# A hand-ordered decoder-layer kernel: five engine queues and their buffer choices replaced by another order

## The chip, the cores and the metric

The kernel runs on one core of one Trainium2 chip. The metric is the device time of one execution in microseconds (us). The core has engines that each work through a queue of their own, in order: PE (TensorE, matrix products), DVE (VectorE), ACT (ScalarE) and POOL (GpSimd) for work on rows, and SP (SyncE), which in this kernel does nothing but start transfers (DMAs). Engines meet through semaphores: an instruction whose input is not there holds back everything that is queued behind it on its engine.

## The reference

One layer of a decoder is computed for a prompt of 512 positions and for 8 sample rows that read paged caches. Both groups share all weights. The core of it:

```python
shift, scale, gate = jnp.split(jax.nn.silu(c) @ w_ada + b_ada, 3, axis=-1)
h = x * (1.0 + scale[:, None, :]) + shift[:, None, :]
parts = jnp.split(h @ w_in, np.cumsum(IN_WIDTHS)[:-1], axis=-1)
...
o_a = nsa_attention(...)      # compressed blocks, selected blocks, window
o_b = moba_attention(...)     # top-3 blocks and the own block
y_a = (o_a.reshape(bsz, t, NSA_WIDTH) * jax.nn.silu(a_z)) @ w_up_a
y_b = (o_b.reshape(bsz, t, MOBA_WIDTH) * jax.nn.silu(b_z)) @ w_up_b
mixed = (jax.nn.sigmoid(m_a) * y_a + jax.nn.sigmoid(m_b) * y_b) @ w_out
x_new = layer_norm(DEEPNORM_ALPHA * x + gate[:, None, :] * mixed, ln_g, ln_b)
```

Two things of it matter here. Nothing can be projected before `shift` and `scale` are known, and these take the whole of `w_ada` for them (8 MB in float32). And the sample rows need scores against the selected-block cache, which lies in pages that the page table names.

## The kernel before, in words

**Numbers.** A float32 product is done as three products of a rounded format: the high part of x times the high and the low part of the weight, and the low part of x times the high part. So each weight tile that lands (`raw`) is cast by ACT to its high part and then subtracted by DVE or POOL to get the low part (`lo`, L366). In trace rows the pair of the two parts is `hl`, and of the modulated input it is `hTh` (high) and `hTl` (low).

**The head.** The modulation is computed in 8 chunks j of 128 channels. For a chunk, two 512 KB pieces of `w_ada` (named `u` or `y`, from `ada_ss`, L574) land; `ada` multiplies them with `cs`, the activated conditioning vector, in 8 small matmuls for each piece (rows s<-u,cs); ACT copies the sums (`a`), PE transposes them (s<-first_in,a), DVE reduces them to shift and scale (`ssh`), and ACT and DVE turn a 260 KB piece of x (from `xT`, names ev, z, tmp) into `hTh` and `hTl`. Then the first three weights (names kc, vc, ks in the code; raw_128, raw_140 and raw_153 from `w_cols`, 512 KB each) are multiplied with each chunk as it comes. `cs`, the identity matrix for the transposes and the bias come with one 110 KB transfer, `first_in` (L660): the constants. Where PE has nothing else, `warm` lets it multiply zeros (e<-zn, L657); 20 of these records stand in the head.

**The body.** The other projections (d<-hTh,hl) make most of PE's work. Between them the queue of PE holds the attention of the prompt (scores s<-kd,q, transposes of probabilities pt<-first_in,p, outputs) and of the sample rows. For these, tiles of selected-block pages (`raw<-slck`: 16 pages of 64 KB for one tile) are multiplied with a padded query (e<-raw,zn, L1469 and L1480 through L351), then window rows (`wink`) and block-attention pages (`mobk`, `mobv`). A page's address is read from the page table by SP itself (the rows TENSOR_LOAD and ISA between DMAs). Results of gates are stored to DRAM and loaded again later (`m_d<-mg`).

**What sets the order.** The functions write the instructions in program order; `line_up` then puts each engine's instructions in the order of a table, `QUEUES`, one string of numbers for each of the five engines, by a chain of order-only dependences. `Pool.tile` looks up in a second table, `SLOTS`, which of its buffers each new tile takes, so which earlier tile must have been used up before a load or a write may start. Waits follow from data and buffers; the tables decide only order and buffer. SP's queue carries every load, so a DMA that waits for a buffer holds back all later ones.

Of the kernel before, what the change touches and what calls it, by code (L numbers as in the profile page):

```python
# [74 lines left out]
for _name, _w in (("ident", 128), ("rowmask", 1), ("ones", 1), ("p16", 1),  # L75
# [16 lines left out]
    "ring.wr": "0123012032130213201231203130130231201302301321012303201032131023231120310",  # L92
# [4 lines left out]
    "ps.s": "01101010010101101010110011010101110101001001010101100101000101001010010111011000011000101010011000110111010110100101100110",  # L97
    "start.a": "01010110",
    "ps.d": "01201120102012000221202101202102120121022021020112120201122100201021020112102210021210211012012110211210210202100121201022112102012021220210"
        "2102",  # L100
    "ring.whl": "012012021021021020210210201201201201201201210212021200210201201201210210201201012010210121012010210210210102120",
    "phi.craw": "10230132012323010213",
# [6 lines left out]
    "at.sm": "012345670123456107234567012354673120546701235467012354670123546701235467012356470123546701235467",  # L109
# [32 lines left out]
1233-1234 1158-1169 1187-1192 1255-1256 1244-1246 1186 1247-1248 1193-1198 1213-1218 1263-1264 1271-1272 1199-1210 1227-1232 1219-1224 1249-1254
1235-1240 1257-1262 1307-1308 1279-1288 1295-1300 1289-1294 1265-1270 1273-1278 1309-1314 1345-1350 1355-1360 1301-1302 1317-1318 1331-1332 1315-1316
1319-1324 1339-1342 1325-1330 1343-1344 1333-1338 1361-1362 1351-1354 1365-1370 1385-1390 1363-1364 1303-1306 1371-1374 1395-1402 1375-1376 1403-1408
1383-1384 1451-1456 1391-1394 1377-1382 1461-1466 1409-1410 1415-1420 1449-1450 1423-1428 1421-1422 1411-1414 1493-1498 1431-1438 1429-1430 1439-1444
1507-1512 1485-1490 1457-1460 1491-1492 1445-1448 1503-1506 1475-1478 1467-1468 1529-1534 1519-1520 1555-1560 1587-1592 1499-1502 1469-1474 1513-1518
1527-1528 1521-1526 1479-1484 1561-1568 1573-1578 1595-1600 1543-1554 1539-1542 1585-1586 1603-1608 1615-1622 1601-1602 1569-1572 1627-1632 1609-1614
1583-1584 1535-1538 1579-1582 1593-1594 1635-1640 1653-1658 1661-1666 1669-1674 1633-1634 1651-1652 1623-1626 1693-1696 1675-1680 1645-1650 1667-1668
1681-1682 1641-1644 1683-1688 1705-1710 1659-1660 1697-1704 1689-1692 1737-1744 1719-1722 1745-1750 1711-1718 1727-1732 1769-1770 1754-1755 1723-1726
1771-1776 1756-1767 1751-1752 1781-1786 1793-1798 1791-1792 1733-1736 1817-1822 1831-1836 1809-1811 1753 1812-1814 1803-1808 1768 1777-1780 1823-1824  # L150
1815-1816 1787-1790 1827-1830 1851-1854 1799-1802 1855-1862 1837-1842 1825-1826 1845-1850 1879-1884 1887-1892 1885-1886 1911-1916 1843-1844 1901-1906
1909-1910 1867-1878 1897-1900 1925-1928 1863-1866 1929-1930 1945-1950 1893-1896 1919-1924 1943-1944 1907-1908 1959-1964 1917-1918 1965-1968 1931-1936
1994-1999 1937-1942 2002-2007 1992-1993 1955-1958 1969-1970 1951-1954 1988-1991 2016-2019 1977-1980 1971-1976 1987 2026-2027 1981-1986 2000-2001
2008-2009 2038-2045 2034-2037 2056-2057 2028-2033 2010-2015 2046-2051 2080-2081 2052-2055 2082-2085 2064-2067 2094-2095 2124-2125 2074-2079 2092-2093
2020-2025 2086-2091 2058-2063 2068-2073 2112-2113 2096-2101 2154-2155 2108-2111 2136-2139 2120-2123 2146-2148 2114-2119 2102-2107 2149-2151 2132-2135
2152-2153 2174-2175 2140-2145 2156-2157 2126-2131 2168-2173 2176-2181 2158-2163 2210-2211 2184-2187 2182-2183 2164-2167 2194-2197 2230-2233 2198-2209
2218-2221 2224-2229 2262-2263 2188-2193 2234-2235 2222-2223 2212-2217 2246-2251 2242-2243 2236-2241 2264-2269 2286-2291 2274-2275 2296-2301 2256-2261
2276-2281 2244-2245 2356-2361 2292-2293 2252-2255 2270-2273 2338-2343 2372-2377 2344-2349 2282-2285 2382-2387 2350-2351 2428-2433 2390-2395 2336-2337
2302-2303 2294-2295 2362-2369 2304-2335 2398-2413 2352-2355 2488-2493 2388-2389 2434-2439 2378-2381 2416-2427 2458-2463 2370-2371 2414-2415 2494-2499
2464-2469 2396-2397 2442-2453 2548-2553 2472-2483 2502-2507 2510-2515 2454-2457 2574-2579 2554-2559 2470-2471 2440-2441 2484-2487 2562-2573 2560-2561  # L160
2580-2585 2508-2509 2500-2501 2516-2547 2677-2692 2609-2620 2590-2597 2633-2634 2602-2607 2621-2626 2586-2589 2627-2632 2635-2640 2663-2664 2608
2598-2601 2651-2662 2641-2646 2780-2781 2695-2700 2665-2670 2647-2650 2719-2724 2701-2706 2671-2676 2707-2718 2725-2730 2693-2694 2766-2767 2748-2753
2731-2746 2754-2759 2798-2799 2760-2765 2788-2791 2747 2768-2773 2792-2797 2800-2805 2816-2818 2876-2877 2774-2779 2782-2787 2833-2834 2806-2815
2827-2832 2825-2826 2844-2849 2835-2840 2856-2861 2841-2842 2894-2895 2850-2851 2819-2824 2843 2862-2869 2852-2855 2888-2893 2918-2919 2896-2901
2920-2925 2870-2875 2878-2887 2936-2939 2902-2903 2930-2935 2904-2917 2940-2941 2926-2929 2964-2969 2942-2947 2956-2963 2952-2955 2948-2951 2979-2980
# [1863 lines left out]
```

## Time and profile before

| what | value |
|---|---|
| times of 3 runs | 593.89, 591.33, 590.1 us, median 591.33 us |
| the profiled execution | 590.68 us, of which its span is 588.9 us |
| busy in the span | PE 573.3 us (97%), PE weight loads 84%, DVE 51%, ACT 49%, POOL 48% |
| mean granted clock of PE | 0.988 |
| moved by DMA | 124.83 MB, 212 GB/s over the span |

The profile is of one execution. Its page gives shares over the whole span; the stages are told apart by asking the trace for stretches of time. A timeline row reads: start, duration, engine, line of the kernel, operation, output<-input, shape, how many in a row (x8), and in brackets the idle time before it with what ended that. Buffer numbers are left out of trace names, so raw<-slck stands for each of the page tiles. Line numbers are those of the kernel before; the changed file is one line longer, so each line below the tables has a number that is higher by one.

### The profile page before, as it was taken

What the parts mean: (1) busy time and instruction counts of PE and PEld (TensorE: products, weight loads), DVE (VectorE), ACT (ScalarE), POOL (GpSimd) and SP (SyncE); (2) the same over time, 40 slices, a digit from 0 to 9 for tenths busy, and PEclk for the clock granted to TensorE, in tenths of its full rate; (3) what the DMA queues carried; (4) which work ended last, traced back from release to release, by engine and by line L of the source; (5) the groups of instructions that cost most, each with busy time, mean ns of one, the idle gap of its engine ahead of it and who ended that gap; (6) DMA issues with size and microseconds to landing.
All of it is one profiled execution on the core that took longest, in us unless ns stands there. A gap on an engine that the chain in (4) does not pass through costs nothing.

```text
span 588.9 us, 13102 instructions
## 1 busy us (share of the span) xinstructions
PE 573.3 (97%) x4672; PEld 493.9 (84%) x4672; DVE 300.2 (51%) x838; ACT 289.4 (49%) x680; POOL 282.8 (48%) x313
## 2 busy tenths in 40 slices
PE   6999999999999899999999999999999999999994
PEld 3789999999997688968779898998778778889774
DVE  0676434625565475545354445775541154644485
ACT  2459455735465455644544474666443342332362
POOL 1124476563254345244425647484444246676716
PEclk7999999999999899999999999999999999999998
DMA  8978845621775834367979472860898988342413
GB/s 305 405 274 284 255 119 176 198 80 39 218 206 166 294 138 162 128 233 229 330 272 311 185 251 60 287 211 20 291 390 259 362 313 293 109 163 96 156 64 146
DMA packets 63667, 124.83 MB, mean 212 GB/s; under 512 B 8114, under 2 KB 25970, under 8 KB 63090
## 3 DMA queue, kind: packets, MB, share of 16 engines
q1 hardware_dynamic: 62194, 119.80, 59.8%
q0 software_dynamic: 1408, 4.20, 2.1%
q8 instruction: 37, 0.61, 0.4%
q14 instruction: 28, 0.23, 0.1%
HBM read 114.38 MB, written 9.58 MB: 210 GB/s over the span
## 4 chain that ended last, share of the span: by engine, by line
PE 93%; DMA 2%; DVE 1%; issue 1%; POOL 1%; SPq 1%; POOLq 0%; ACT 0%; DVEq 0%
PE d L351 55%; PE s L351 13%; PE e L351 9%; PE o L351 6%; PE pt L354 5%; PE pt L351 2%; DMA u<-ada_ss 1%; DMA raw<-slck 1%; PE d L354 1%; PE e L354 1%; PE s L354 0%; POOL p L1279 0%; SPq L357 0%; POOL hl L366 0%; SPq L574 0%
## 5 line engine op out<-in xcount | busy, mean ns | idle before, releaser
L351 PE MATMUL d<-hTh,hl 128*128 128x260 f32 (+1 forms) x1392 | 264.1, 287 | 0.0
L351 PEld LDWEIGHTS d<-hTh,hl 128*128 128x128 f32 (+1 forms) x1392 | 215.7, 188 | 2.4 <-issue 0.8
L351 PE MATMUL d<-hTl,hl 128*128 128x260 f32 (+1 forms) x704 | 198.2, 282 | 0.0
L351 PEld LDWEIGHTS d<-hTl,hl 128*128 128x128 f32 (+1 forms) x704 | 131.7, 187 | 0.0
L366 POOL TENSOR_TENSOR hl<-raw,hl 128x512 fp32r<-128x512 f32 x56 | 73.6, 1315 | 105.5 <-ACT hl L448 86.3
L1277 ACT ACTIVATE p<-s,sm 128x512 f32<-128x512 f32 (+3 forms) x96 | 50.6, 529 | 69.0 <-DVE sm L1274 45.5
L448 ACT CAST hl<-raw 128x512 fp32r<-128x512 f32 (+1 forms) x103 | 62.7, 618 | 44.2 <-PE d L351 20.2
L1279 POOL TENSOR_SCALAR p<-p,sm,gp 128x512 f32<-128x512 f32 (+3 forms) x64 | 42.8, 677 | 75.9 <-DVE sm L1278 68.9
L351 PE MATMUL d<-yh,hl 128*128 128x260 f32 x256 | 47.7, 286 | 0.0
L366 DVE TENSOR_TENSOR hl<-raw,hl 128x512 fp32r<-128x512 f32 (+1 forms) x47 | 37.1, 791 | 18.0 <-ACT hl L448 17.1
L351 PEld LDWEIGHTS d<-yh,hl 128*128 128x128 f32 x256 | 40.1, 188 | 4.0 <-issue 2.1
L354 PE MATMUL pt<-first_in,p 128*128 128x128 f32 x240 | 39.9, 281 | 0.8 <-DVE pp L1287 0.8
L354 PEld LDWEIGHTS pt<-first_in,p 128*128 128x128 f32 x240 | 27.4, 142 | 14.4 <-issue 9.0
L1287 ACT COPY pp<-pt 128x512 f32<-128x512 f32 (+1 forms) x48 | 23.0, 479 | 28.0 <-PE pt L354 27.7
L1274 DVE CUSTOM_DVE_ANT_0 s<-s,band 128x256 f32<-128x256 f32 (+1 forms) x48 | 17.3, 364 | 37.9 <-PE s L351 31.6
L351 PE MATMUL d<-yl,hl 128*128 128x260 f32 x128 | 36.2, 282 | 0.0
L1279 POOL TENSOR_SCALAR p<-p,sm,first_in 128x128 f32<-128x128 f32 (+3 forms) x32 | 23.8, 751 | 25.0 <-DVE sm L1278 24.7
L1272 DVE TENSOR_REDUCE sm<-s 128x1 f32<-128x256 f32 (+1 forms) x48 | 16.9, 355 | 33.2 <-PE s L351 27.0
L351 PE MATMUL s<-kd,q 128*128 128x512 f32 (+3 forms) x96 | 32.1, 337 | 0.0
L1287 DVE COPY pp<-pt 128x512 f32<-128x512 f32 x24 | 16.5, 688 | 28.3 <-PE pt L354 22.9
L351 PE MATMUL s<-kd,qx 128*128 128x512 f32 (+3 forms) x96 | 30.8, 323 | 0.0
L366 POOL TENSOR_TENSOR u<-craw,u 128x512 fp32r<-128x512 f32 x16 | 21.7, 1360 | 17.1 <-DMA craw<-cmp 5.9
(415 smaller groups left out, 1062.3 us busy)
## 6 DMA issues: line engine op xcount, KB each, us to landing
raw<-w_cols SPq DMA_DIRECT2D x46, 512.0 KB
raw<-mobk SPq DMA_DIRECT2D x64, 256.0 KB
raw<-mobv SPq DMA_DIRECT2D x64, 256.0 KB
craw<-cmp SPq DMA_DIRECT2D x64, 128.0 KB
u<-ada_ss SPq DMA_DIRECT2D x12, 512.0 KB
raw<-slck SPq DMA_DIRECT2D x64, 64.0 KB
raw<-ada_g SPq DMA_DIRECT2D x8, 512.0 KB
raw<-w_up SPq DMA_DIRECT2D x8, 512.0 KB
```

Of the source, the lines that this page charges most:

```text
L351: return mmraw(out, lhsT, rhs, start=start, stop=stop, skip_group_check=True)
L354: return nc.tensor.transpose(out, x, unit)
L366: (nc.gpsimd if eng == "p" else nc.vector).tensor_sub(out, x, f32(hi))
L448: nc.scalar.copy(h, src)
L1272: nc.vector.tensor_reduce(sm[:, 0:1], s[:, :b], axis=AX, op=OP.min)
L1274: nc.vector.tensor_tensor_reduce(out=s[:, b:n], in0=s[:, b:n], in1=j.band[:, 256 - (n - b):], scale=1.0, scalar=top, op0=OP.add, op1=OP.mi ...
L1277: nc.scalar.activation(pr, s[:, :n], AF.Exp, scale=-1.0, bias=sm[:, 1:2], accum_out=sm[:, 2:3])
L1279: D.setdefault("pool", []).append(nc.gpsimd.tensor_scalar(pr, pr, sm[:, 3:4], j.gate(i), op0=OP.mult, op1=OP.mult))
L1287: j.copied[gi] = (nc.scalar.copy if COPY_ENG[gi] == "a" else nc.vector.tensor_copy)(t[:, :n], p[:, :n])
```

## The change

Every instruction and every operand stays as it was. The tables `QUEUES` (all five engines) and `SLOTS` (six of its strings) hold other numbers. Cut to one of the strings and the first numbers of one queue:

```diff
 SLOTS = {
     "phi.u": "010101010100",
-    "ring.wr": "0123012032130213201231203130130231201302301321012303201032101031023231120310",
+    "ring.wr": "2013012302130210321301302102102302130321320310212303201023232103012203132",
...
 QUEUES = {
     "PE": """
-0-3 5-12 20-27 4 13 34-35 14-19 42-45 39-41 46-49 31-33 36-38 58-60 56-57 64-66 92-94 28-30 70-77 67-69 95-97 84-85 50-52 78-80 61-63 89-91 53-55
...
```

The numbers tell a reader nothing, so here is what stands in the queues.

**SP's queue at the start of the program.** `u_114` is the buffer of chunks 0 and 1 of `ada_ss` (the first two pieces are chunk 0, the next two chunk 1), `u_150` that of chunks 2 and 3; ev_136 and z_148 are the pieces of x for chunks 0 and 1. Before:

```order
L574 DMA u_114<-ada_ss 128x1024
L660 DMA first_in_72<-first 128x219
L574 DMA u_114<-ada_ss 128x1024 x3
L357 DMA raw_128<-w_cols 128x1024
L701 DMA pos_106<-pos 128x32
L357 DMA raw_140<-w_cols 128x1024
L702 DMA ptt_76<-pt 1x64
L559 DMA ev_136<-xT 128x520
L559 DMA z_148<-xT 128x520
L574 DMA u_150<-ada_ss 128x1024 x2
L357 DMA raw_153<-w_cols 128x1024
```

and now:

```order
L575 DMA u_114<-ada_ss 128x1024 x2
L358 DMA raw_128<-w_cols 128x1024
L661 DMA first_in_72<-first 128x219
L575 DMA u_114<-ada_ss 128x1024 x2
L702 DMA pos_106<-pos 128x32
L560 DMA z_148<-xT 128x520
L560 DMA ev_136<-xT 128x520
L703 DMA ptt_76<-pt 1x64
L575 DMA u_150<-ada_ss 128x1024
L358 DMA raw_140<-w_cols 128x1024
L575 DMA u_150<-ada_ss 128x1024 x2
L358 DMA raw_153<-w_cols 128x1024
```

The constants go from second to fourth place, behind another 512 KB piece of `ada_ss` and the weight raw_128; both pieces of x and the second weight change places.

**PE's queue at the start.** s_181 and s_211 are the sums of chunks 0 and 1, s_258 those of chunk 2, kd_142 is the second weight (raw_140) and v2_130 the first (raw_128). Before:

```order
L351 MATMUL e_112<-zn_90 128x256 x4
L351 MATMUL s_181<-u_114,cs_75 32x256 x8
L351 MATMUL s_211<-u_114,cs_75 32x256 x8
L351 MATMUL e_112<-zn_90 128x256 x2
L354 MATMUL s_211<-first_in_72,a_237 128x128 x2
L354 MATMUL s_181<-first_in_72,a_191 128x128 x2
L351 MATMUL e_112<-zn_90 128x256 x4
L351 MATMUL s_258<-u_150,cs_75 32x256 x4
L351 MATMUL o_251<-hTh_73,kd_142 128x260 x2
```

and now:

```order
L352 MATMUL e_112<-zn_90 128x256 x8
L352 MATMUL s_181<-u_114,cs_75 32x256 x4
L352 MATMUL s_211<-u_114,cs_75 32x256 x4
L352 MATMUL s_181<-u_114,cs_75 32x256 x4
L355 MATMUL s_181<-first_in_72,a_191 128x128 x2
L352 MATMUL s_211<-u_114,cs_75 32x256 x4
L355 MATMUL s_211<-first_in_72,a_237 128x128 x2
L352 MATMUL e_112<-zn_90 128x256 x2
L352 MATMUL d_230<-hTh_73,v2_130 128x260 x2
```

Eight of the ten products of zeros now stand ahead of everything, and the transposes of chunk 0 go between the pieces of chunk 1. (One zero product is two records in the trace; a group of 8 s<-u,cs records there is the x4 of one piece.)

**SP's queue where the last tile of selected-block pages is loaded** (raw_2783, 16 pages in four groups, each group behind a read of the page table; raw_2959, raw_2509 and raw_2721 are weight tiles, mg and ev rows that are stored). The rows with pages that only repeat are cut. Before:

```order
L357 DMA raw_2783<-slck 128x128
L357 DMA m_d_94<-mg_2504 128x520
L928 TENSOR_LOAD ptt_76
...
L357 DMA ok<-ev_2171 128x520
...
L357 DMA m_d_94<-mg_2716 128x520
L357 DMA raw_2959<-w_cols 128x1024
...
L357 DMA raw_2981<-wink 128x2048
```

and now:

```order
L358 DMA raw_2783<-slck 128x128
L358 DMA raw_2509<-w_cols 128x1024
L929 TENSOR_LOAD ptt_76
...
L358 DMA raw_2783<-slck 128x128
L358 DMA raw_2981<-wink 128x2048
L358 DMA m_d_94<-mg_2716 128x520
L358 DMA m_d_94<-mg_2944 128x520
L358 DMA band_3094<-band 128x512
L358 DMA raw_2721<-w_cols 128x1024
```

Before, a store stood behind the first group, another behind the second, and a store and a 512 KB weight behind the third, ahead of the last four pages. Now a weight stands behind the first group and nothing between the others; the store of mg_2504 stands ahead of the tile, the stores of mg_2716 and ev_2171 behind it, and so do the weights raw_2721 (which stood far ahead) and raw_2959 (now behind the store of mg_3102).

Elsewhere PE's queue is nearly the same; DVE's adds a step to `cvd_539` (L1077) ahead of the choice of selected blocks (dn, L1108) instead of behind it, and the transposes pt_4898 in PE's queue stand behind projections that they stood ahead of.

More of the change, by code (lines that the diff above doesn't have):

```diff
@@ L96 @@
     "kv.kl": "01",
-    "ps.s": "01101010010101101010110011010101110101001001010101100101000101001010010111011000011000101010011000110111010110100101100110",
+    "ps.s": "01010101101010010101001100101010001010110110100101100101000011001101101000100111100111010101011000110110101001100110100101",
     "start.a": "01010110",
[L99 to L102, printed above, removed]
+    "ps.d": "01201021012012022001202101202102120121000201202110102021100211012110201220210102210102100201201020122120120102100121200122010121201210112102"
+        "0120",
+    "ring.whl": "012012021021021201201201210210210210210210201212021022012012012012021020120120201202102012021020120120120201210",
+    "phi.craw": "10320132102323012301",
     "phi.sst": "0",
@@ L108 @@
     "at.mg": "01010101010101",
-    "at.sm": "012345670123456107234567012354673120546701235467012354670123546701235467012356470123546701235467",
+    "at.sm": "012345670123456102734567012354673120546701235467012354670123546701235467012356470123546701235467",
     "at.p3": "010101010101010101010101",
@@ L230 @@
[L230 to L233 removed]
+0-4 13 16-17 5-8 20-23 9-12 14-15 24-27 34-35 18-19 31-33 28-30 39-49 70-73 56-57 36-38 58-60 74-77 67-69 95-97 84-85 64-66 92-94 61-63 89-91 53-55
@@ new lines @@
+81-83 50-52 78-80 123-125 151-153 126-129 98-101 130-133 102-105 109-111 140-141 112-113 106-108 120-122 148-150 117-119 154-161 86-88 114-116 168-169
+134-136 179-181 145-147 176-178 204-206 182-189 142-144 170-172 196-197 207-209 225-227 162-164 190-192 137-139 165-167 193-195 213-215 210-212
+173-175 201-203 198-200 216-218 231-233 222-224 228-230 219-221 246-257 234-245 270-275 258-269 276-281 298-303 282-287 314-317 288-297 304-313
+330-341 318-329 343-348 355-360 342 361-366 349-354 384-395 461-472 372-377 367-371 430-432 378-383 433-438 406-417 396-399 418-420 439-444 421-426
@@ new lines @@
+457 400-405 427-429 445-447 485-490 448-450 458-460 451-456 473-478 491-496 479-484 497-502 509-520 551-559 533-538 560-565 503-508 521-532 566-568
+575-577 581-586 578-580 605-610 569-574 587-598 611-616 599-601 617-622 602-604 629-640 653-658 623-628 641-652 696-701 665-670 744-749 671-676
+702-704 659-664 705-710 677-682 750-755 690-695 756-761 720-722 539-541 711-719 542-550 723-743 768-785 762-767 786-797 804-815 798-803 816-821
+829-840 883-894 841-846 895-900 847-849 901-906 919-924 683-685 850-852 907-912 859-861 686-687 913-918 688-689 950-955 862-870 956-961 925-930
@@ new lines @@
+2713-2718 2735-2740 2748-2753 2741-2746 2754-2759 2798-2799 2760-2765 2768-2773 2792-2797 2788-2791 2800-2805 2816-2818 2747 2876-2877 2774-2779
+2782-2787 2833-2834 2806-2815 2819-2824 2827-2832 2841-2842 2894-2895 2825-2826 2844-2849 2856-2861 2835-2840 2850-2851 2870-2875 2843 2862-2869
+2852-2855 2888-2893 2918-2919 2896-2901 2878-2881 2920-2925 2904-2905 2882-2887 2930-2935 2902-2903 2906-2917 2940-2941 2926-2929 2936-2939 2942-2947
+2964-2969 2973-2978 2962-2963 2952-2961 2948-2951 2971-2972 2979-2980 3003-3008 3021-3026 3001-3002 2981-2986 2991-2996 2970 3051-3056 2987-2990
@@ new lines @@
+4030-4041 3994-3996 3988-3990 4003-4005 4000-4002 4055-4057 3997-3999 4014-4017 4098-4100 4058-4069 4077-4082 4042-4045 4083-4097 4122-4124 4070-4073
+4101-4103 4125-4127 4104-4106 4128-4130 4107-4115 4131-4133 4116-4118 4134-4136 4119-4121 4137-4145""",
+    "Activation": """
+0 7 1 10 8-9 3 11 4 12 5 14 13 15 6 2 18 16-17 20 19 21-22 26 23 25 24 31 30 54 39 27 35 34 33 32 28 53 38 43 36-37 45 44 46 48 47 41 52 40 55 59 62
+57 42 60 67 61 58 49 66 64 50 56 65 51 69 68 63 80 79 70 76 83 86 77 81 78 87 29 71 85 90 84 89 82 72 101 95 99 108 88 102 73 104 100 109 103 75 96
@@ new lines @@
+390 396 402 401 404 403 411 421 400 409 406 410 413 405 415 387 428 417 408 414 418 412 456 422 416 429 427 419 426 431 425 423-424 430 434 437
+432-433 436 441 435 438 440 439 444 450 442 445 443 446 455 453 447 449 407 452 458 451 459-461 448 457 462 466 464 454 465 474 470 482 475 463 469
+468 467 473 471-472 480 476 478 487 479 481 486 488 493 477 483 492 495 489 499 484 498 490 496 500 494 491 485 502 501 508 504 513 512 510 503 505
+511 506 509 497 507 514 516-517 519 515 521 520 522 518 524 523 527 525 528 531 530 529 526 534 532 535 537 539 533 538 541 540 536 542 545 544 543
@@ new lines @@
+603 596 601 593 600 602 604 597 599 606 605 607 610 612 608 613-614 611 618 616-617 615 623 609 619 626 620 624 622 627-628 625 630 629 632 631 633
+638 634-636 639-640 637 641 645 642 644 649 646 648 650 653 643 654 647 652 651 656-657 655 659-660 658 664-665 662 669 668 661 666 663 667 671 679
+673 672 680 670 675 674 677-678 684 683 676 682 681 685-686 688-689 687 703 690 705 692 704 691 696 709 699 710 693 702 698 706 694 711 707 716 708
+718 717 695 712 721 713 723 722 700 714 697 701 715 725 727 719 726 720 728 730 729 724 731-736 739 738 737 741 740""",
+    "Pool": """
@@ new lines @@
+184 130 181 189 179 185 178 187 182-183 131 186 190 204 193-194 188 191 195 192 197 205 198-199 201 156 196 210 206 208 207 211 209 216 203 202
+214-215 217 213 221 219 225 218 224 226 220 212 223 228 231 230 229 227 238 232 222 233 236 235 237 234 242-243 246 241 245 247 239 251 253 240 252
+244 248-250 257 254 256 255 260 258-259 261 264 297 262 268 270 263 269 265 267 271 266 275 272-273 279 282 274 280 276 281 277 283 278 286 284 290
+292 291 285 295 287 289 293 296 294 288 298-299 302 300 303 301 304-308""",
+    "SP": """
@@ new lines @@
+1 5 3 0 2 6 31 8 4 32 9 7 10 13 11 14 12 16 15 19-20 17-18 22-23 21 25-26 24 38 27 33 37 41-45 39 48 40 50 49 47 51-55 62 56 28 57-61 63-67 69-73 30
+74-78 81-90 68 80 36 29 35 79 91-95 97-101 96 102-106 108-112 107 119 114-118 34 130 120-129 131-136 138 137 144 147-151 139 152-161 141 113 143 140
+162-166 142 167-171 173-177 172 179-183 146 185-189 178 190-195 239 196-205 207-216 184 218-232 234 217 235 237 206 236 240-244 46 296 245 233 238
+251-252 246-250 253 145 267 257-266 269-273 268 255 274-278 256 279-283 285-289 295 254 290-294 297-301 303-312 302 314-318 320-324 326-330 284
@@ L234 @@
+332-336 325 319 313 337 339 341 331 344-345 354 351 343 353 346-350 361 352 338 355-360 365 342 364 367 363 340 445 370-374 368 366 375-379 369
+380-390 419 392-401 403-407 391 408-417 402 432 468 418 420-429 443 433-442 448-452 431 430 444 473 453 447 498 465 458 456 362 495 455 466-467 469
+446 462 493 492 457 454 470 460 464 496 472 459 475-476 463 471 461 474 478 481 479-480 484 482 477 483 489 486 485 488 487 494 491 499 497 490 500
+507 501 505 503 502 506 508 504 510 509 511""",
 }
```

164 lines of the change are left out of this document (64 added, 100 removed).

## Prediction

> **What bounds the kernel now.** I read the page first: which engine is full, and which work stands in the chain of waits that ended last.
>
> ```profile
> PE 573.3 (97%) x4672; PEld 493.9 (84%) x4672; DVE 300.2 (51%) x838; ACT 289.4 (49%) x680; POOL 282.8 (48%) x313
> PE 93%; DMA 2%; DVE 1%; issue 1%; POOL 1%; SPq 1%; POOLq 0%; ACT 0%; DVEq 0%
> ```
>
> PE is busy for 573.3 of 588.9 us, so at most 15.6 us of its idle time could go, and no other engine comes near. All instructions stay, so only three things can move the end: idle time of PE, time in which its clock was halved, and records that fill time but compute nothing. The waits of PE, longest first:
>
> ```profile
> PE s L351 <- DMA u<-ada_ss: 2.8, 3, 2.4
> PE e L351 <- DMA raw<-slck: 1.9, 1, 1.9
> ```
>
> (total us, times, longest). The first is in the head, the second near 200 us; what else there is stands in rows below. Then stretches of PE, cut where the granted clock changes; columns are the stretch, PE's busy time, the clock, the DMA engines' busy share and GB/s:
>
> ```profile
> 4.60:8.03 3.43, 1.50 (x17) 1.00 0.84 258
> 8.03:11.44 3.41, 1.83 (x16) 0.50 1.02 405
> 11.44:14.86 3.42, 3.42 (x14) 0.50 1.04 413
> 14.86:18.27 3.41, 3.27 (x27) 1.00 1.03 408
> 199.18:202.59 3.41, 1.47 (x13) 1.00 0.99 392
> 202.59:206.00 3.41, 3.41 (x15) 0.50 1.00 383
> 20.00:36.00 16.00, 15.97 (x165) 1.00 1.04 402
> ```
>
> The clock changes in steps of 3.41 us, and each stretch's clock answers to how busy PE was in the one before: 1.50, 1.83 and 1.47 us busy are followed by half clock, 3.42 us by full. So a wait of 1.9 us costs more than itself. From 20 to 36 us PE has no wait though DMA is full: there the pieces of `ada_ss` arrive just in time.
>
> **The head.** PE's and ACT's rows there:
>
> ```profile
> 1.10 3.71 PE L351 MATMUL e<-zn 128*128 128x256 f32 x8 [1.10 <-POOL zn L663]
> 5.53 0.64 PE L351 MATMUL s<-u,cs 128*32 128x256 f32 x8 [0.71 <-DVE cs L671]
> 9.45 1.08 PE L351 MATMUL s<-u,cs 128*32 128x256 f32 x8 [2.37 <-DMA u<-ada_ss]
> 10.69 1.08 PE L351 MATMUL s<-u,cs 128*32 128x256 f32 x8 [0.16 <-DMA u<-ada_ss]
> 13.57 1.06 PE L354 MATMUL s<-first_in,a 128*128 128x128 f32 x4
> 14.43 2.11 PE L351 MATMUL e<-zn 128*128 128x256 f32 x8
> 17.24 0.48 PE L351 MATMUL o<-hTh,kd 128*128 128x260 f32 x2
> 4.63 0.26 ACT L669 ACTIVATE sc<-first_in 128x72 f32<-128x72 f32 x1 [2.61 <-DMA first_in<-first]
> 11.98 0.62 ACT L639 CAST v<-raw 128x512 fp32r<-128x512 f32 x1 [4.47 <-DMA raw<-w_cols]
> 12.50 0.37 ACT L588 COPY a<-s 128x256 f32<-128x256 f32 x1
> 13.33 0.62 ACT L639 CAST kd<-raw 128x512 fp32r<-128x512 f32 x1 [0.47 <-DMA raw<-w_cols]
> 15.64 0.60 ACT L604 ACTIVATE hTh<-ev,ssh 128x252 fp32r<-128x252 f32 x1 [1.17 <-DVE ssh L592]
> ```
>
> The first projection starts at 17.24 us. A transfer's arrival goes by the bytes ahead of it: at 9.45 three 512 KB pieces and the 110 KB of constants are there, at 10.69 four, at 11.98 five, at 13.33 six. In the new order the constants are fourth, behind exactly three such pieces: they land near 9.4 instead of 4.63 us. From there to PE's first real product it took 0.9 us (4.63 to 5.53), so PE begins at 10.35. The last piece of chunk 1 is fifth, near 12.0; both pieces of x, 260 KB each, come next, near 13.3.
>
> Eight zero records of 0.46 us, then eight of 0.25 (2.03 us for x8 from 14.43 to the next row of PE), fill PE to 6.9; it idles until 10.35. So 8.03 to 11.44 is mostly idle and 11.44 to 14.86 runs at half clock. Whether 8.03 to 11.44 is full is open: 2.3 us busy lies between 1.83 and 3.42. At half clock: three pieces at 1.08 end at 13.6; copy 0.37, two transposes 0.5: 14.5; the fourth piece, mostly at full clock: 15.3; copy 0.37 and transposes at full clock: 16.0; four zero records at 0.25: 17.0, the first projection. If 8.03 to 11.44 is full, 0.6 less: 16.4. `hTh` of chunk 0 is no later: its transposes end at 14.5, shift and scale 0.5 later, the activation 0.6 later again. Before, PE had also done one piece of chunk 2 by 17.24, worth 0.64, so equal progress comes at 17.0 to 17.6. I take **+0.2 us**. Bounds: all at full clock, 10.35 + 4 x 0.64 + copies and transposes 1.2 + zeros 1.0 + 0.64 = 15.75, **-1.5**; half clock also in 14.86 to 18.27, another 1.7 lost, **+2.0**. Less than -1.5 is excluded by the bytes: the pieces up to chunk 7 sum to the same, on engines that are full.
>
> The Trainium skill ("TensorE: Matmul & The Clock Gate", Part 1) says that the gate falls to half after an idle window of about 3.4 us. By that rule the idle 6.9 to 10.35, which fills no window, would halve nothing, and the head would reach the lower bound. The rows above disagree: half clock followed windows with 1.5 to 1.8 us of work.
>
> **The last selected-block tile.** PE's rows and the transfer in the chain of waits; then SP's issues:
>
> ```profile
> 199.34 1.06 PE L351 MATMUL e<-raw,zn 128*32 128x512 f32 x8
> 202.35 2.17 PE L351 MATMUL e<-raw,zn 128*32 128x512 f32 x8 [1.94 <-DMA raw<-slck]
> 195.96 6.15 DMA raw<-slck
> ```
>
> ```profile
> 184.34 2.53 SPq L357 DMA_DIRECT2D raw<-slck  x4
> 186.91 0.43 SPq L357 DMA_DIRECT2D m_d<-mg  x1
> 187.89 1.88 SPq L357 DMA_DIRECT2D raw<-slck  x4
> 189.82 0.43 SPq L357 DMA_DIRECT2D ok<-ev  x1
> 190.78 1.88 SPq L357 DMA_DIRECT2D raw<-slck  x4
> 192.76 0.38 SPq L357 DMA_DIRECT2D m_d<-mg  x1
> 193.24 0.37 SPq L357 DMA_DIRECT2D raw<-w_cols  x1
> 194.40 1.89 SPq L357 DMA_DIRECT2D raw<-slck  x4
> ```
>
> The pages are wanted at 200.4 and land at 202.1, because the last is issued at 195.96. The gaps between the four groups are 1.0, 1.0 and 1.75 us; without the two stores, and with a weight in one gap alone, they are about 1.0, 0.55 and 0.55, so the last issue comes 1.65 earlier, at 194.3. With the same 6.15 us to landing it is there at 200.45, as PE wants it; but those 6.15 us held a 512 KB weight issued 2.7 us ahead (1.3 us of DMA, by the spacing 9.45, 10.69, 11.98), which now goes much earlier. So the wait goes: **-1.9** (bounds 0 and -1.9). Next late is nothing here: PE's own queue. With the wait goes the half clock of 202.59 to 206.00, in which half the work was done: **-1.7** (0 to -1.7; it stays whole if a wait of over half a window is left). By the same page no 1.9 us wait would halve the clock, and this term would be nothing; the rows at 199.18 and 202.59 show that it does.
>
> What was moved out must still be in time. Weights raw_2721 and raw_2959 are now issued after the tile; their casts:
>
> ```profile
> 211.68 1.30 ACT L448 CAST hl<-raw 128x512 fp32r<-128x512 f32 x2 [0.46 <-ACT p L1277]
> 223.36 0.62 ACT L448 CAST hl<-raw 128x512 fp32r<-128x512 f32 x1
> 215.57 0.80 SPq L357 DMA_DIRECT2D m_d<-mg  x2
> ```
>
> raw_2721 is issued near 198 for 211.68: covered. raw_2959 stands behind the store that waited until 215.57, so it goes near 216 for 223.36: 7 us, over the 6.15 above. Cost nothing, with 1 us of cover. Queued behind that store on SP are three weights and the next block pages.
>
> **Two small waits.**
>
> ```profile
> 148.80 0.38 PE L351 MATMUL e<-first_in,pr 128*128 128x1 f32 x2 [0.37 <-DVE ocmp L1168]
> 336.07 0.66 PE L354 MATMUL pt<-first_in,p 128*128 128x128 f32 x4 [0.79 <-DVE pp L1287]
> 19.03 0.40 PE L351 MATMUL d<-hTh,kd 128*128 128x260 f32 x2
> 19.39 0.40 PE L351 MATMUL d<-hTh,kd 128*128 128x260 f32 x2
> ```
>
> Near 336 the transposes wait 0.79 for a copy. They now stand behind four more groups of three projections, 0.36 each (19.03 to 19.39): 1.4 us of cover, **-0.8** (0 to -0.8). Near 148 one DVE step goes ahead, but the copy waited for stays behind the choice of blocks: **-0.2** (-0.6 to +0.5).
>
> **New waits.** Five queues were dealt anew with other buffers; the trace can't show a wait that isn't there yet. Nearest rows: 0.8 (near 336) and 1.9 plus 1.7 of clock. I take one of the small kind, **+0.8**, bounds 0 and +4. Everything else, including the end after PE's last product, keeps its place.
>
> Sum: +0.2 -1.9 -1.7 -0.2 -0.8 +0.8 = -3.6, on the profiled execution's 590.68: 587.1. Its time is 0.65 under the median of the runs; I forecast **587.0 us**.
>
> **Rivals.**
> (a) *The late constants cost.* PE stays at half clock until 18.27: 2.0 instead of 0.2, 588.9. For it: the window 11.44 to 14.86 has gaps for copies. Against: some 3.0 of its 3.41 us are busy, nearer to 3.42 than to 1.83.
> (b) *The tile is late anyway.* Its pages land behind other traffic, and both terms stay: 590.7. Against: less stands ahead.
> (c) *Slower: the weight behind the store.* raw_2959 and the two weights behind it all wait for one store on SP. If the casts come late, PE stands at its product, wanted about 4 us after the cast, and pays the lateness plus 1.7 of clock. Past 223.4 it costs; against the gains of 3.6 it decides from 2 us late on; at 10 us late the time is 599. For: 1 us of cover by the longest landing in the trace. Against: that landing was with DMA full.
> (d) *All idle goes and the head gains.* Terms at their lower ends: -1.5 -1.9 -1.7 -0.6 -0.8, no new wait: 584.2.
>
> **How the numbers follow.** Forecast 0.52 (585.0 to 589), (a) 0.14, (b) 0.12, (c) 0.11, (d) 0.11. The range runs from 583, just under (d), to 594, which takes in (a), (b) and a mild (c). About 1% (5.9 us) can be told from no change. Below 585.4: (d) and the low part of the forecast, 0.11 + 0.13 = 0.24. Above 597.2: most of (c), 0.09. Between: 0.67.
>
> **What would show it.** PE's first projection between 16.3 and 17.1, with half clock at 11.44 to 14.86 and full after; no PE wait on raw<-slck and no half clock near 200; no wait for pp near 336; SP's last page issued about 10 us after the first. It is wrong if PE waits for a cast near 227, or if half clock shows anywhere after 20 us.

## The result, and the profile after

| | kernel before | changed kernel |
|---|---|---|
| median of 20 runs each | 590.02 us (585.53 to 593.89) | 586.25 us (584.44 to 588.88) |
| the profiled execution | 590.68 us, span 588.9 | 588.88 us, span 587.1 |
| ratio, 95% interval | | 0.9949 [0.9934, 0.9964] |

So the change is worth about 3 us, 0.5%, less than 1%. The profiled execution of the changed kernel is the slowest of its 20 (2.6 us above their median), so the pair of first traces shows only 1.8 us. This matters below: the waits differ from one execution to the next, and a second trace of each kernel was taken.

The page of the changed kernel: busy engines, then the chain of waits by engine.

```profile
PE 569.3 (97%) x4672; PEld 493.2 (84%) x4672; DVE 306.7 (52%) x838; ACT 288.2 (49%) x680; POOL 280.9 (48%) x313
PE 85%; DMA 7%; SPq 3%; DVE 2%; issue 1%; ACT 1%; POOL 0%; POOLq 0%; DVEq 0%; ACTq 0%
```

PE's busy time, which includes slow records, fell by 4.0 us; its idle time rose by 2.2. The waits of PE are other ones (total us, times, longest):

```profile
PE s L352 <- DVE cs L672: 2.5, 1, 2.5
PE e L352 <- DVE ocmp L1169: 1.7, 1, 1.7
PE e L352 <- POOL zn L664: 1.1, 1, 1.1
PE s L352 <- ACT u L1038: 1.0, 1, 1.0
PE s L355 <- ACT a L589: 1.0, 2, 0.5
PE d L352 <- DVE hTl L612: 0.7, 1, 0.7
PE s L352 <- DMA u<-ada_ss: 0.6, 1, 0.6
```

The wait for raw<-slck and the wait for pp are gone; a wait for `ocmp` (a DVE copy of what the compressed blocks give the sample rows) near 150 us and one for a cast `u` near 94 us are new. PE's rows in the head, and two stretches of it (stretch, PE busy, clock, DMA share, GB/s):

```profile
1.10 5.49 PE L352 MATMUL e<-zn 128*128 128x256 f32 x16 [1.10 <-POOL zn L664]
9.11 1.50 PE L352 MATMUL s<-u,cs 128*32 128x256 f32 x24 [2.51 <-DVE cs L672]
11.47 0.64 PE L352 MATMUL s<-u,cs 128*32 128x256 f32 x8
13.83 0.50 PE L352 MATMUL d<-hTh,v 128*128 128x260 f32 x2
19.89 0.64 PE L352 MATMUL s<-u,cs 128*32 128x256 f32 x8 [0.56 <-DMA u<-ada_ss]
4.60:8.03 3.43, 2.00 (x9) 1.00 1.00 340
8.03:11.44 3.41, 1.84 (x26) 1.00 1.02 394
```

The first projection starts at 13.83 instead of 17.24 us and from 4.7 us on nothing in the head runs at half clock in this trace.

Where the time went can be followed by pairing PE's work in two traces: for each row of the one, when the other had done as much (work counted with the smaller spacing that each matmul found in both had in either trace; another way of matching them moves the values by up to 0.7 us). Changed kernel minus kernel before, us:

| at (us of before) | first traces | second traces |
|---|---|---|
| 20 | -1.7 | -1.1 |
| 63 | -1.0 | -1.8 |
| 94 | -0.5 | -1.9 |
| 106 (first), 113 (second) | +1.3 | -1.6 |
| 162 (first), 172 (second) | +3.6 | -0.9 |
| 195 | +3.1 | -1.3 |
| 220 | -0.8 | -5.0 |
| 345 (first), 352 (second) | -1.8 | -5.1 |
| 482 | -1.3 | -3.9 |
| 555 | -1.5 | -4.2 |

In both pairs one place, 195 to 220 us, is worth 3.7 to 3.9 us, and places between 94 and 172 us give some of it back, 4.1 us in the first pair and 1.0 in the second.

### The profile page after: what moved, and what is told of

It reads as the page before. It is cut to its first block, busy times and chain, and to the rows that moved or that the text cites. A ratio compares the mean times of both kernels' runs of the same rounds, so it can differ in the third digit from the quotient of the medians.

```text
span 587.1 us, 13119 instructions
## 1 busy us (share of the span) xinstructions
PE 569.3 (97%) x4672; PEld 493.2 (84%) x4672; DVE 306.7 (52%) x838; ACT 288.2 (49%) x680; POOL 280.9 (48%) x313
## 4 chain that ended last, share of the span: by engine, by line
PE 85%; DMA 7%; SPq 3%; DVE 2%; issue 1%; ACT 1%; POOL 0%; POOLq 0%; DVEq 0%; ACTq 0%
PE d L352 51%; PE s L352 11%; PE e L352 8%; PE o L352 7%; PE pt L355 5%; SPq L358 2%; DMA u<-ada_ss 2%; PE pt L352 2%; DMA y<-ada_ss 2%; DMA raw<-ada_g 1%; DMA craw<-cmp 1%; DMA tab<-tab 1%; PE e L355 1%; PE d L355 1%; ACT u L1038 0%
## 5 line engine op out<-in xcount | busy, mean ns | idle before, releaser
L1278 ACT ACTIVATE p<-s,sm 128x384 f32<-128x384 f32 (+3 forms) x96 | 50.7, 530 | 59.0 <-DVE sm L1275 39.9
L1280 POOL TENSOR_SCALAR p<-p,sm,gp 128x128 f32<-128x128 f32 (+3 forms) x64 | 41.8, 661 | 66.9 <-DVE sm L1279 59.1
L367 DVE TENSOR_TENSOR hl<-raw,hl 128x512 fp32r<-128x512 f32 (+1 forms) x47 | 40.9, 871 | 16.0 <-ACT hl L449 15.7
L1280 POOL TENSOR_SCALAR p<-p,sm,first_in 128x256 f32<-128x256 f32 (+3 forms) x32 | 21.7, 683 | 27.0 <-DVE sm L1279 23.4
L1273 DVE TENSOR_REDUCE sm<-s 128x1 f32<-128x128 f32 (+1 forms) x48 | 17.0, 354 | 29.4 <-PE s L352 29.0
L352 PE MATMUL s<-kd,q 128*128 128x256 f32 (+3 forms) x96 | 31.3, 329 | 0.0
L352 PE MATMUL s<-u,w1h 128*128 128x256 f32 (+1 forms) x128 | 29.0, 292 | 1.6 <-ACT u L1038 1.0
L352 PE MATMUL s<-kd,qx 128*128 128x256 f32 (+3 forms) x96 | 30.2, 321 | 0.0
```

The source lines that it names most:

```text
L352: return mmraw(out, lhsT, rhs, start=start, stop=stop, skip_group_check=True)
L367: (nc.gpsimd if eng == "p" else nc.vector).tensor_sub(out, x, f32(hi))
L1273: nc.vector.tensor_reduce(sm[:, 0:1], s[:, :b], axis=AX, op=OP.min)
L1278: nc.scalar.activation(pr, s[:, :n], AF.Exp, scale=-1.0, bias=sm[:, 1:2], accum_out=sm[:, 2:3])
L1280: D.setdefault("pool", []).append(nc.gpsimd.tensor_scalar(pr, pr, sm[:, 3:4], j.gate(i), op0=OP.mult, op1=OP.mult))
```

## The experiments

The theory from the prediction: the gain comes from the last tile of selected-block pages, whose issue and landing were late. The first rival: the head. Each experiment's edit is in the tables of order alone; the diffs below name the instructions that it moves. Names with b_ are made from the kernel before, those with a_ from the changed kernel; the line numbers in their rows can be one or two lower. The medians come from four chips, on which the kernel before had 588.79 to 590.08 us, so kernels are compared by the ratio to the kernel before on the same chip; it isn't the quotient of the two medians and can differ from that by 0.001. Each median is of 12 executions, those of a_dve, a_cmp and a_best of 7, 9 and 6.

| run | median us | ratio, 95% interval |
|---|---|---|
| b_pages | 588.93 | 0.9995 [0.9972, 1.0017] |
| b_weight | 588.77 | 0.9997 [0.9982, 1.0011] |
| b_head | 589.11 | 0.9997 [0.9980, 1.0014] |
| b_band | 589.48 | 0.9995 [0.9971, 1.0020] |
| b_both | 589.16 | 0.9981 [0.9951, 1.0010] |
| after_again | 586.53 | 0.9965 [0.9943, 0.9987] |
| a_dve | 585.72 | 0.9941 [0.9920, 0.9962] |
| a_cmp | 585.58 | 0.9946 [0.9926, 0.9966] |
| a_oldhead | 587.56 | 0.9988 [0.9969, 1.0007] |
| a_oldpages | 587.45 | 0.9963 [0.9944, 0.9982] |
| a_best | 583.68 | 0.9903 [0.9881, 0.9925] |

### The pages alone, in the kernel before

```diff
 DMA raw_2783<-slck            (pages 5 to 8)
-DMA ok<-ev_2171
 DMA raw_2783<-slck            (pages 9 to 12)
-DMA m_d<-mg_2716
-DMA raw_2959<-w_cols
 DMA raw_2783<-slck            (pages 13 to 16)
+DMA ok<-ev_2171
+DMA m_d<-mg_2716
+DMA raw_2959<-w_cols
 DMA raw_2981<-wink
```

> The kernel before, and in SP's queue alone the stores of mg_2716 and ev_2171 and the weight raw_2959 are put behind the last page of raw_2783; all else, buffers too, as before. Theory (what stood among and ahead of the pages made them late): PE's wait for raw<-slck of 1.9 us and the half clock behind it go, 3.6 to 4 us less, 0.994 of before. Rival (the gain near 200 us came from other buffers or from PE coming 3 us later): PE still waits over 1 us for raw<-slck, time within 1 us of before.

In b_weight only the last of the three, the weight, is moved.

> The kernel before, and only the weight raw_2959 is put behind the last page of raw_2783, both stores stay among the pages. Theory A (the 512 KB ahead of the last four pages make them land 6.15 us after their issue): the last page lands about 2 us after its issue, near 198, no wait, the same gain as with the stores moved too. Theory B (the issue gaps count): the last page is issued only 0.5 us earlier, PE still waits 1.4 us and the clock is halved in some runs.

Both traces did what the theory says. PE's row at the tile, of the one and of the other kernel:

```profile
200.06 1.92 PE L350 MATMUL e<-raw,zn 128*32 128x512 f32 x16
```

```profile
200.88 1.93 PE L350 MATMUL e<-raw,zn 128*32 128x512 f32 x16
```

All 16 products run through, without a wait and at full clock, as theory A of b_weight says for the weight alone. By the pairing both traces are 4.0 us better between 190 and 220 us than the first trace of before. But the times did not move: 0.9995 and 0.9997, where 0.994 was expected. Two cautions: the traced execution was the second fastest of the twelve in both kernels (587.03 and 587.92 us), and no trace shows a slower one. And the pages were in time in the second trace of the kernel before too, with nothing moved (next section), so these rows alone don't show that moving the weight was enough.

### The kernel before and the changed kernel once more

> The kernel before once more, unchanged, for a second trace of it. If the wait for raw<-slck near 200 us belongs to every execution, it is there again with 1.5 to 2.5 us and the half clock behind it; if it came from how the transfers fell in that one execution, it is under 0.5 us. The same for the 0.8 us wait for pp near 336 us.

> The changed kernel once more, unchanged, for a second trace and for its time beside the runs of this call. 0.995 of before. If the waits for ocmp near 150 us and for the cast near 94 us belong to the order, they are there again with 1.7 and 1.0 us; the half clock behind the first comes only where the 3.4 us stretches fall so that one is less than half busy.

In the second trace of the kernel before (589.84 us) the pages are in time. The row that is late stands one place further on: the chain of waits, PE's row, and PE's stretches there (stretch, PE busy, clock, DMA share, GB/s).

```profile
198.26 9.17 DMA band<-band
209.22 0.66 PE L351 MATMUL s<-kd,q 128*128 128x384 f32 x1 [1.90 <-ACT p L1277]
206.40:209.80 3.40, 1.50 (x10) 0.92 0.64 263
209.80:213.20 3.40, 3.40 (x19) 0.58 0.04 18
```

The band table (256 KB, wanted by DVE at once) was issued behind pages, a 512 KB weight, 1 MB of window rows and a store, and took 9.17 us; softmax, and so PE, waited 1.9 us, and the clock was halved for 3.4 us. The same loss as in the first trace, from another transfer. A trace of b_head has it too, with 10.24 us for the band, a wait of 2.2 us and 3.4 us at half clock. The wait for pp near 336 us was in the first trace of before and not in the second: it isn't a property of the order alone.

The second trace of the changed kernel (585.38 us) has the wait for ocmp of 1.7 us again, but no half clock behind it, and no wait near 94 us.

### The band ahead of the window rows, in the kernel before

```diff
 DMA raw_2783<-slck            (page 16; no store or weight among the pages)
+DMA m_d<-mg_2716
+DMA ok<-ev_2171
+DMA m_d<-mg_2944
+DMA band_3094<-band
 DMA raw_2981<-wink
-DMA m_d<-mg_2944
-DMA band_3094<-band
 DMA raw_3086<-wink
+DMA raw_2959<-w_cols
```

> The kernel before, and in SP's queue alone near 185 to 202 us: the stores of mg_2716 and ev_2171 behind the last page of raw_2783, then the band table band_3094, and only then the 1 MB of window rows raw_2981 and the weight raw_2959. Theory (before pays one late transfer between 199 and 210 us in every execution, either the pages or, behind them, the band; moving the pages alone shifts the wait to the band): neither wait shows, and 2 to 4 us less in the median, 0.9935 to 0.9965 of before. Rival (the loss near 200 us belongs to few executions): within 1 us of before, as with the pages moved alone.

Neither wait was in its trace (587.36 us), yet the time is 0.9995 [0.9971, 1.0020]: the rival's number. That closes the simple form of the theory: taking the loss near 200 us away, both forms of it, is not by itself worth 2 us or more in the median of the kernel before.

The traces alone would say otherwise. By the pairing, each of the three with the old order there (both of before, and b_head) loses some 4 us between 190 and 220 us, and none of the four in which the weight or more was moved does (b_pages, b_weight, b_band, b_both). But the traced execution of b_band was again a fast one, the fastest of twelve. The mean granted clock, which is kept for every execution, gives no sign of a saved half clock: 0.9926 over the 36 executions of b_pages, b_weight and b_band, 0.9932 over the 50 of the kernel before on the same chips, where 3.4 us less at half clock would add 0.003. Why the medians don't follow the traces stays open.

### The pages put back, in the changed kernel

The reverse of b_pages: the two stores and raw_2959 stand among the pages again.

> The changed kernel, and in SP's queue alone the weight raw_2959 and the stores of mg_2716 and ev_2171 go back among the pages of raw_2783 as they stood before. Theory: PE waits again near 200 to 210 us, for the pages or the band, and 1.5 to 3.5 us of the gain go, 0.998 to 1.001 of before. Rival (the gain lies elsewhere): 0.995 to 0.9965 as the changed kernel.

The wait came back (the chain of waits and PE's row):

```profile
197.08 3.39 DMA raw<-slck
200.51 1.28 PE L351 MATMUL e<-raw,zn 128*32 128x512 f32 x8 [0.81 <-DMA raw<-slck]
```

It costs 0.8 us there and no clock. The time, 0.9963, lies between the two ratios of the changed kernel, 0.9949 and 0.9965: the rival's number again. So 0 to 0.8 us of the gain hang on this place; the intervals allow more.

### The head alone, and the head put back

In b_head the instructions of about the first 24 us stand in the new order (for SP and PE as shown with the change above); in a_oldhead they are put back. POOL's queue is left alone in both, which turns out to matter.

> The kernel before, and on all five engines the instructions of about the first 24 us put in the order of the changed kernel (constants fourth, eight zero products first, first weight kc); all later ones and all buffers as before. Theory (the gain of the changed kernel is made in the head: first projection near 14 instead of 17 us, no half clock): 1.5 to 3 us under before, 0.995 to 0.9975. Rival (the head is paced by the arrival of the pieces of ada_ss up to 34 us, an earlier start is given back): within 0.8 us of before.

> The changed kernel, and on all five engines the instructions of about the first 24 us put back in the order of before. Theory (head): the gain falls to 0 to 1.5 us, 0.9975 to 1.0 of before. Rival (the gain lies in the later queues): 0.995 as the changed kernel. The half clock from 8 to 15 us comes back in either case.

b_head did not gain: 0.9997. But its head is not that of the changed kernel. The low part of the first weight (`v`) is made in two halves. In b_head ACT casts both ahead of `hTh`, POOL subtracts one and DVE the other, side by side:

```profile
11.14 1.14 ACT L638 CAST v<-raw 128x512 fp32r<-128x512 f32 x2
11.85 1.27 POOL L365 TENSOR_TENSOR v<-raw,v 128x512 fp32r<-128x512 f32 x1 [10.28 <-ACT v L638]
12.31 1.35 DVE L365 TENSOR_TENSOR v<-raw,v 128x512 fp32r<-128x512 f32 x1 [2.99 <-ACT v L638]
```

In the changed kernel one half is made there, and the other after 24 us:

```profile
10.94 0.62 ACT L640 CAST v<-raw 128x512 fp32r<-128x512 f32 x1
11.60 0.69 DVE L367 TENSOR_TENSOR v<-raw,v 128x512 fp32r<-128x512 f32 x1 [2.47 <-ACT v L640]
26.43 1.27 POOL L367 TENSOR_TENSOR v<-raw,v 128x512 fp32r<-128x512 f32 x1
```

So DVE starts 0.7 us later on it and needs 0.7 us more, and shift, scale, `hTh` and PE's first projections behind them come 1.4 us later than in the changed kernel's trace. PE's rows, and two stretches of it:

```profile
15.21 0.50 PE L350 MATMUL d<-hTh,v 128*128 128x260 f32 x2 [1.10 <-ACT hTh L603]
16.45 0.39 PE L350 MATMUL d<-hTl,v 128*128 128x260 f32 x1 [0.73 <-DVE hTl L610]
13.41:16.82 3.41, 1.57 (x9) 1.00 1.02 408
16.82:20.23 3.41, 3.41 (x27) 0.50 1.03 406
```

With these waits a stretch is less than half busy, and PE runs at half clock up to 20.23 us. By 30 us the kernel stood where before_again stood (+0.2). That is the number of b_head's rival but not its cause: PE has no wait for `ada_ss` of 0.2 us or more in this trace. b_head doesn't tell what the changed kernel's head is worth.

a_oldhead is at 0.9988, in the range of the head theory (0.9975 to 1.0), and its interval leaves out the rival's 0.995. On the same chip the changed kernel (after_again) is at 0.9965. So with the head undone 1.0 us of 2.3 is lost by the medians, 1.4 us of 2.1 by the ratios. Their intervals overlap; an estimate from the 12 times of each kernel (means 587.86 and 586.65 us) gives 1.2 us, 0.1 to 2.3 us with 95% if the executions are independent. The expected half clock came too, and for longer:

```profile
5.55 1.08 PE L351 MATMUL s<-u,cs 128*32 128x256 f32 x8 [0.66 <-DVE cs L671]
8.93 1.08 PE L351 MATMUL s<-u,cs 128*32 128x256 f32 x8 [2.29 <-DMA u<-ada_ss]
12.86 2.08 PE L351 MATMUL e<-zn 128*128 128x256 f32 x4
18.73 0.50 PE L351 MATMUL o<-hTh,kd 128*128 128x260 f32 x2
```

A piece takes 1.08 us instead of 0.64, and four zero records 2.08 instead of 1.03. The clock column of the views doesn't show this: it reads 1.00 up to the first change of clock that was recorded, here at 17.11 us. By the pairing this trace is 2.9 us behind the second trace of the changed kernel at 34 us and 2.8 us at 345: nothing is given back up to there. The other traces agree in kind. At 63 us the six with the changed kernel's head are 0.7 to 1.0 us ahead of the first trace of before, and the other four with the head of before level with it to 1.5 us behind.

### Both parts together

b_both has the head of b_head, so not quite the changed kernel's either, and the SP order of b_band.

> The kernel before with both parts that alone moved nothing: the head of about 24 us in the changed kernel's order on five engines, and near 185 to 202 us pages, stores and band ahead of window rows and weight. Theory A (the two parts pay only together, since what one saves the other place takes back): 1.5 to 3 us under before, 0.995 to 0.9975. Theory B (the gain of the changed kernel is spread over its queues between and behind these places): within 1 us of before, 0.9985 to 1.0015.

0.9981 [0.9951, 1.0010], inconclusive: its point lies between the theories and its interval holds both.

### The new waits of the changed kernel

```diff
 DVE im_2075            (L1163)
-DVE kd_1354<-ev_1350   (low part, L367)
 DVE lst_2080
 DVE dn_92              (choice of blocks)
...
 DVE ocmp_93<-e_2125
 DVE dn_92
+DVE kd_1354<-ev_1350
```

> The changed kernel, and in DVE's queue alone the low part kd_1354 (from ev_1350, 1.67 us) is put behind the choice of blocks (dn) near 151 us. Theory (this step in the chain makes the 1.7 us wait for ocmp and so the half clock behind it): the wait falls under 0.4 us, no half clock there, about 2.4 us under the changed kernel, 0.991 of before. Rival (POOL working at the same time slows whatever stands there): dn and pr take over 1 us each as in the kernel before, the wait stays over 1 us, under 0.8 us gained.

In the changed kernel DVE and POOL did this near 148 us, then PE:

```profile
147.31 1.67 DVE L367 TENSOR_TENSOR kd<-ev,kd 64x512 fp32r<-64x512 f32 x1
149.22 0.92 DVE L1109 SCALAR_TENSOR_TENSOR dn<-im,lst,cstd 128x14 f32<-128x14 f32 x1
150.55 0.28 DVE L1169 COPY ocmp<-e 128x128 f32<-128x128 f32 x1
147.12 1.31 POOL L1228 TENSOR_TENSOR q<-y,q 64x512 fp32r<-64x512 f32 x1 [1.45 <-ACT q L1226]
148.51 1.60 POOL L1230 TENSOR_TENSOR qx<-y,q 64x512 fp32r<-64x512 f32 x1
150.88 0.38 PE L352 MATMUL e<-first_in,pr 128*128 128x1 f32 x2 [1.74 <-DVE ocmp L1169]
148.10:151.52 3.42, 1.68 (x14) 1.00 0.48 133
151.52:154.94 3.42, 3.42 (x18) 0.50 0.00 0
```

With kd_1354 behind the chain the wait fell to 1.0, not under 0.4, because another step, the copy gc, now ran beside POOL:

```profile
146.99 1.31 POOL L1229 TENSOR_TENSOR qx<-y,q 64x512 fp32r<-64x512 f32 x1
147.19 1.14 DVE L823 COPY gc<-gp 128x8 f32<-128x8 f32 x1
148.65 0.38 PE L351 MATMUL e<-first_in,pr 128*128 128x1 f32 x2 [1.04 <-DVE ocmp L1168]
```

The rival comes closer: the wait stays over 1 us, though dn (0.95 us) and gc were held up and not pr. There is no half clock behind it, but after_again, with the whole wait, has none either. The time, 0.9941, can't be told from the changed kernel's 0.9949.

```diff
 DMA raw_1054<-w_cols
+DMA raw_1168<-w_cols
...
 DMA craw_1287<-cmp            (page 4)
-DMA raw_1168<-w_cols
 DMA craw_1326<-cmp
```

> The changed kernel, and in SP's queue alone the weight raw_1168 goes back out of the compressed pages, behind raw_1054 near 70 us. Theory (its 512 KB among the pages make craw_1378 land 4.4 instead of 3.1 us after its last issue): PE's 1.0 us wait for the cast u near 94 us falls to 0.3 or less, about 1.3 us under the changed kernel. Rival (the two weights issued right behind the pages share the engines with them): the wait stays, no change.

The wait near 94 us was not in its trace; but it was not in the second trace of the changed kernel either, and the time is 0.9946. What made the wait in the first trace stays open.

### A faster version

a_best has the second of these edits; on DVE it puts pr_2018 and the copy ocmp ahead of lst and dn and kd_1354 behind; on SP it puts band_3094 and raw_2721 right behind the last page, ahead of stores and window rows.

> The changed kernel with three of its waits taken away: on DVE the copy ocmp ahead of the choice of blocks and the low part kd_1354 behind it; on SP the weight raw_1168 out of the compressed pages; on SP the band table and the weight raw_2721 ahead of stores and window rows. Theory: the wait for ocmp of 1.7 us and its half clock go, the wait near 94 us stays under 0.3 us: 1.5 to 3 us under the changed kernel, 0.990 to 0.993 of before. Rival (waits move on to transfers near 415 and 470 us): within 1 us of the changed kernel.

It runs at 583.68 us, 0.9903 [0.9881, 0.9925]; its interval lies under both intervals of the changed kernel (taken on other chips), so it beats both kernels. Near 148 us nothing is left of the wait for ocmp, and a wait of 0.4 us for the next step is new:

```profile
146.48 0.29 DVE L1168 COPY ocmp<-e 128x128 f32<-128x128 f32 x1
146.95 0.28 PE L351 MATMUL e<-first_in,pr 128*128 128x1 f32 x2
149.20 0.38 PE L351 MATMUL e<-first_in,pr 128*128 128x1 f32 x2 [0.42 <-DVE snew L1127]
```

By PE's paired work it is 2.0 us ahead of the second trace of the changed kernel at 150 us, relative to where it stood at 113, and 1.3 us at 162. Another 1.3 us come between 345 and 482 us, where that trace waits 0.8 us for raw<-mobv; the spans are 581.2 and 583.6 us. Which of its three edits carries what was not tried apart from a_dve and a_cmp.

## Why the prediction was right, and where it was not

The number held: 587.0 us forecast, 586.25 measured, inside 583 to 594, and the likeliest of the three classes, within 1%, came. That it came so near is partly luck: terms that were off in size or sign cancelled. Two of the prediction's own signs failed, the head's (first projection between 16.3 and 17.1 us, half clock at 11.44 to 14.86) and "half clock shows anywhere after 20 us", which it named as a sign of being wrong: the first trace of the changed kernel has it at 151.5 to 154.9 us.

**The head, +0.2 taken.** Mis-sized: -1.0 in the first traces by 63 us, inside the bounds. Two steps failed. The constants landed earlier than the bytes said (ACT started on them at 8.21 instead of 9.4 and PE at 9.11, not 10.35; DMA was 1.00 busy from 4.60 to 8.03 instead of 0.84, with the small transfers further back). And no half clock came at 11.44 to 14.86. I had read the row "8.03:11.44, 1.83, 0.50" as a window with too little work; but that window ran at half clock itself. At full clock, windows with 1.84 and 2.00 us of work kept the clock, and 1.47, 1.50 and 1.68 lost it. The part that held is the pacing: 1.7 us ahead at 20 us, 1.0 at 63, with PE's wait for `ada_ss` at 19.89. But the head is not as small a term as taken: in a_oldhead about half of the gain went with it.

**The clock rule of the Trainium skill** ("TensorE: Matmul & The Clock Gate", Part 1: half after an idle window of about 3.4 us) was rejected in the prediction. The rows still speak against it as far as waits of 1.7 to 2.2 us halved the clock in five traces (both of before, b_head, the first of the changed kernel, a_cmp), without an idle window; for the head its outcome, no half clock, was the one that came.

**The last tile, -1.9 and -1.7.** Place and size were right in the traces: 3.9 us there in the first pair, 3.7 in the second, where the loss came from the band. The step "so the last issue comes 1.65 earlier" held and more: 9.3 us from first to last page instead of 11.6. The larger part was the landing: the last page, issued at 198.64, was in by 200.5, 1.9 us later instead of 6.15. That the weight ahead of it made the difference is likely but not shown, since the pages were in time in before_again with the weight in its place. What failed is to take the wait of a traced execution as a price of the median: b_pages and b_band had it no more in their traces, and their medians stayed. In the changed kernel, putting the order back cost 0 to 0.8 us.

**Near 148, -0.2.** Wrong in sign: +1.3 us of wait, and 1.7 of half clock in the first trace. I had weighed the step that moved ahead of the chain and not kd_1354, which had moved into it, and took 1.67 us where 0.69 stood before.

**Near 336, -0.8.** The wait was gone, but it was also gone in the second trace of the kernel before, and back with 0.9 in those of b_band and b_both. It comes and goes.

**New waits, +0.8.** Right in kind: 1.3 us near 94 and 0.3 near 471 in the first trace; the second has 0.8 for raw<-mobv instead.

**Rivals.** (a) did not come: both traces of the changed kernel keep the clock in the head. a_best, with the same head, ran at half clock from 9.86 to 13.27 and was level with after_again (0.15 us behind) by 34 us. (b) did not come in the traces of the changed kernel, where the pages are in time. (c) did not come: PE has no wait near 227, raw_2959 behind the store was in time. (d) was not reached by the changed kernel; a_best is near it.

So the sum was right, although its two largest terms can't be shown in the time and one of its smallest, the head, seems to carry about half of what was measured: 1.0 to 1.4 of 2.1 to 2.3 us on one chip, with an estimated interval that just leaves out zero, and as far as the head of a_oldhead, without POOL's part, stands for that of the kernel before. The pages undone cost 0 to 0.8 us. The rest was not taken apart, and the head alone, with POOL's and ACT's share of it, was not tried in the kernel before.

## What to carry to other kernels

A wait that ends in a transfer can come from another transfer in the next execution, and taking it away need not show in the median: before costing its removal, look at a second trace of the same kernel, ask which transfer behind it is next late when the queue is as full, and see where the traced execution stands among the others. On a queue of loads, look at what stands ahead of a small table that is wanted next: behind 1 MB of window rows the band took 9 to 10 us in two traces, ahead of them PE didn't wait for it in b_band's trace, though the median stayed. In a chain that PE waits for, look at what was moved into it as much as at what was moved out. When a stage is carried over to another kernel, carry every engine's part: here one half of a weight that stayed in front on POOL and ACT cost 1.4 us in the trace of b_head. And read a clock from how long equal instructions take, not from the clock column alone.

## What the runs showed of the hardware

POOL and DVE hold each other up. A DVE copy of 128x8 (gc) that took 0.17 us in the changed kernel took 1.14 in a_dve, ending at 148.33 with POOL's operation (146.99 to 148.30). The kd step, 0.69 us elsewhere, took 1.67 and ended 0.55 us after the POOL operation that it had started beside (147.12 to 148.43); the next on POOL took 1.60 instead of 1.31. In b_head the same happened to v: 1.35 instead of 0.69 us, ending 0.54 us after POOL's. The Trainium skill says so ("GPSIMD Engine Reference", section 8: it shares its SBUF interfaces with VectorE and contends with instructions of two SBUF inputs or in a two-port mode). The rows of kd and v, with two inputs each, agree; the copy has one, and no run shows in which mode it ran.

A wait decides PE's clock by where it falls. The clock changes in steps of 3.41 us, and the same wait for ocmp of 1.7 us halved the clock in two traces (1.68 us of work in that step in the changed kernel, 1.67 in a_cmp) and not in three (1.71 in after_again, 1.91 in a_oldpages, and in a_oldhead, where it fell across two steps with 2.88 and 2.20). Over all 14 traces, steps at full clock with at most 1.58 us of work were followed by half clock, those with 1.7 or more were not, and between them both occurred: the border is near half a step.
